# Feed-forward stage of a streaming encoder step: paced weight sums, operands of the first down steps on other bytes, sample columns stored apart, sums moved to POOL

## The chip, the cores and the metric

The kernel runs on one core of one Trainium2 chip. The metric is the device time of one execution in microseconds. Before the change the median of three runs is 1256.84 us (1256.39 to 1259.03). The engines are PE (TensorE, matrix products), DVE (VectorE), ACT (ScalarE), POOL (GpSimd) and SP (SyncE, which here issues the DMA transfers). Each engine works through its own instructions in order; they wait for one another by semaphores.

## The reference, cut to what matters

One layer of a hybrid encoder is computed for 1024 prompt frames and 8 × 16 sample frames: windowed attention and a state-space branch, an output projection, and then a feed-forward block with a short convolution. Only this last block is touched by the change:

```python
def conv_ffn(x, prev, w_up, conv_w, conv_b, w_down):
    up = x @ w_up                                        # 1152 rows, 1024 -> 2 * 2816
    up_p = jnp.concatenate([prev.astype(up.dtype), up], axis=1)
    c = sum(up_p[:, j:j + L] * conv_w[j] for j in range(CONV_W)) + conv_b
    gate, val = jnp.split(c, 2, axis=-1)
    return (jax.nn.silu(gate) * val) @ w_down, up_p[:, -(CONV_W - 1):]

x = x + f                                                # then the final rmsnorm
```

All tensors are float32. The last two rows before the convolution are an output too (conv_prompt, conv_sample).

## The kernel before

**Precision and products.** Every float32 operand is split into a high part (ACT: a copy to fp32r) and a low part (DVE: source minus high part); a product is three matmuls, high × high, high × low and low × high (`mm3`, lines 61 to 63). Every DVE tensor_tensor goes through the helper `tt`, so all of them stand at line 86 and are told apart by their tiles. Both matrix products of the block use a Strassen-like scheme: seven products of blocks in place of eight, with sums and differences of operands formed beforehand.

**Up stage.** The loop at line 1451 runs over 22 pairs j. A pair is 128 gate columns and 128 value columns. `load_up` brings its weights in (tiles `ur`, three buffers, 512 KB each). `prep(n)` makes operand n = 7j + i: POOL forms the sums of weights (`S`, and in place in `ur`, line 1253), ACT and DVE split them into `op` (lines 1297 and 1298). It runs seven operands, one pair, ahead of the products. `product(n, g)` does 12 matmuls for each of two groups of token tiles (g = 0: 320 columns, g = 1: 256) into PSUM tiles `pu{j}{g}{bank}`. `collect` moves the results to the row buffer `ext`, by ACT copies (line 1357) or DVE adds. `up_pair_end(j - 1)` does the convolution (`up_conv`: ACT line 1387, DVE lines 1388 and 1389), the SiLU (line 1394) and the product of gate and value, and stores the finished rows g to DRAM (`g_d`, line 1398): 1024 prompt columns and 144 columns of the samples (8 × (16 + 2)).

**Weight sums.** The down stage needs four sums of blocks of w_down. They are formed during the up stage, in 22 chunks: `wd_load(i)` loads four blocks of 256 columns into the one buffer `ws` (two DMAs, line 1414), `wd_sums(i)` does four DVE subtractions in place and stores the chunk to `t_d` (line 1424). In the loop the sums of chunk j - 1 are written at i == 0 and the load of chunk j at i == 3. Because `ws` has one buffer, a load has to wait until the store before it has landed.

**Down stage.** After the up stage its pools are closed, and new ones take the same bytes: `gr0` and `dwA` on the left, where the up weights (`upW`), the operands `op` with i < 3 (`opL`) and the split activations of group 0 (`hA`) lay, in this order, and `gr` and `dw` on the right. Seven passes of 11 steps follow (B11, T1, T2, B22, T3, B21, T4). A step loads a block of weights (`w_op`, tiles `wd`, five buffers), splits it (`wh`, `wl`), splits a tile of g (`gh`, `gl`), and does 12 matmuls for four tiles of prompt rows (`dna`, `dnb`). The first pass (line 1601) also takes the sample columns: four weight blocks a step, and 12 more matmuls for the 128 sample rows (`dns`). Two loads a step bring the sample columns of g (`gs`, line 1497). The pass for T1 needs `SU[k]`, the sum of two g tiles: `sum_one`, on DVE. `conv_out` transposes the convolution's last rows on PE (`cvo`, line 1549) and writes them out. `half_one` and `half_two` do the final normalization of a tile; for the samples they are written in pass T2 at step 3, and `final_g` (`fgb`) is loaded in T1 at step 9.

**What sets the order.** The program is written in one order, and a planner with a cost model then puts each engine's instructions into the order in which it expects them to be ready; the written order is the priority among ready ones. `with tc.issue_after(x):` adds an edge: the instructions of the block that run on the engine of x are queued behind x. It adds no semaphore. A tile of a pool can be written when all accesses of the tile that had its bytes are done.

Of the kernel before, what the change touches and what calls it, by code (L numbers as in the profile page):

```python
# [18 lines left out]
P = 128  # L19
# [26 lines left out]
def emit(ctx, tc, x_prompt, x_sample, cache_k, cache_v, state_ssm_re, state_ssm_im, state_conv,  # L46
# [1221 lines left out]
    RAW, OPS = {}, {}  # L1268

    def load_up(j):  # L1270

        if j < NF:
            for i in range(2):
                raw = upW.tile([P, 2, 4, P], F32, name=f"ur{j}{i}", tag="ur", bufs=3)
                c = i * DF + j * P
                nc.sync.dma_start(raw, w_up[0, :, c:c + P].rearrange("(h k p) n -> p h k n", p=P, h=2))
                RAW[j, i] = raw
# [6 lines left out]
    def prep(n):  # L1284
# [13 lines left out]
        tt(op[:, 1], src, f(op[:, 0]), OP.subtract)  # L1298
# [68 lines left out]
    g_d = dram.tile([NF, P, GLEN], F32, name="g_d")  # L1367
# [23 lines left out]
    def up_pair_end(j):  # L1391
# [6 lines left out]
        nc.sync.dma_start(g_d[j], g)  # L1398
# [52 lines left out]
    for j in range(1, NF):  # L1451
        load_up(j + 1)
        up_begin(j)
        for i in range(7):
# [7 lines left out]
            if i == 0:  # L1462
                wd_sums(j - 1)
            if i == 3:
                wd_load(j)
# [20 lines left out]
    def load_g(h, q, k):  # L1486

        if k < NK:
            pl = gr0 if h == q == 0 and k < 4 else gr
# [40 lines left out]

    load_g(0, 0, 0)
    load_g(0, 0, 1)
    load_gs(0)
    load_g(0, 0, 2)
    load_g(0, 0, 3)
    load_gs(1)
    for k in range(NK):
        SU[k] = None
# [59 lines left out]


    smb = {}  # L1600
    for k in range(NK):
        w = {}
        for blk in ("B11", "B12", "B21", "B22"):
            w[blk] = w_op(blk, k)
            if blk == "B11":
                g = g_op(GA[0, 0, k])
                pairs("a", k, g, w[blk], True)
                if k == 0:
                    smb = {e: pdn.tile([P, 512], F32, name=f"dns{e}", tag=f"b{2 + e}") for e in range(2)}
                sm = []  # L1610
                for q in range(2):
                    v = GS[q, k].rearrange("p (b s) -> p b s", s=NS + 2)[:, :, 2:]
                    hi, lo = (dwA.tile([P, P], F32R, name=f"s{x}{q}{k}", tag=f"s{x}{q}", bufs=2) for x in "hl")
                    hv, lv = (z.rearrange("p (b s) -> p b s", s=NS) for z in (hi, lo))
                    act(hv, v, AF.Copy)
                    tt(lv, v, f(hv), OP.subtract)
                    sm.append((hi, lo))
# [135 lines left out]
```

## Time and profile before

| | |
|---|---|
| median of 3 runs | 1256.84 us |
| profiled execution, its own time | 1257.5 us |
| its span in the profile | 1255.7 us |
| mean granted clock of TensorE | 0.974 |
| busy PE / DVE / ACT / POOL | 93% / 75% / 52% / 18% |
| up stage, pairs 2 to 20, in the span | 504.6 to 957.6 us |
| last matmul of the up stage ends | 986.35 us |
| last matmul of the down stage ends | 1242.3 us |

A row of a timeline holds the start in us, the duration in us, engine, line, operation, tiles (out<-in), shapes, how many were merged, and in brackets the idle time of the engine before it with what ended it. In a row of a chain the start is followed by the duration and what worked. A row of a table by windows holds the window and its length, then the busy time (and number of instructions) of PE, PEld (weight loads into PE), DVE, ACT and POOL, the granted clock of TensorE, the busy share of the DMA engines and GB/s. A row of a group holds line, engine, operation, tiles, shapes, count, then busy us, mean ns of one, and the idle time just before them with its causes. DMA issues stand at SPq. PE's rows overlap a little, since matmuls are pipelined; the distance between starts is the true pace. The span counts from the first instruction, and the execution's own time is a little longer.

### The profile page before, as it was taken

How to read it: one execution, taken by the hardware profiler on the slowest of the kernel's cores; microseconds unless marked ns; L12 is line 12 of the kernel's file. 1: busy time of each engine (PE TensorE's matmuls, PEld its weight loads, DVE VectorE, ACT ScalarE, POOL GpSimd, SP SyncE). 2: the span in 40 equal slices, each digit the busy share in tenths (PEclk: the TensorE clock that was granted, in tenths of full speed). 3: DMA queues.
4: the chain of work that ended last, by engine and by line, in shares of the span. 5: the costliest groups of instructions: out<-in, count | busy, mean ns of one | idle time of the engine just before them, and what ended most of it. 6: DMA issues, size and time to landing. Idle time of an engine off the chain costs nothing.

```text
span 1255.7 us, 20729 instructions
## 1 busy us (share of the span) xinstructions
PE 1172.0 (93%) x7396; PEld 1031.3 (82%) x7396; DVE 945.7 (75%) x2159; ACT 653.2 (52%) x1414; POOL 228.3 (18%) x276
## 2 busy tenths in 40 slices
PE   8999999999979878998899889999999899999995
PEld 6777776777878678998899889999999777888884
DVE  6898778888258888777787787776767669977666
ACT  7346557653467675443444344545454455546553
POOL 0000000000000114333443345553634000000000
PEclk9999999999999888999999999999999899999998
DMA  7523247638622433354534452212222499943333
GB/s 249 106 99 106 96 110 221 202 129 239 202 72 99 154 101 102 121 172 147 161 121 161 140 162 73 87 63 81 70 73 70 154 312 327 332 135 94 100 92 134
DMA packets 163945, 177.90 MB, mean 142 GB/s; under 512 B 30554, under 2 KB 121314, under 8 KB 163810
## 3 DMA queue, kind: packets, MB, share of 16 engines
q1 hardware_dynamic: 163842, 176.58, 44.7%
q8 instruction: 58, 0.95, 0.3%
q14 instruction: 45, 0.37, 0.1%
HBM read 124.36 MB, written 53.23 MB: 141 GB/s over the span
## 4 chain that ended last, share of the span: by engine, by line
PE 53%; DVE 19%; DMA 15%; issue 5%; ACT 5%; SPq 3%; POOL 1%; DVEq 0%; ACTq 0%; POOLq 0%
DMA ws<-in_w_down_dram 5%; DMA t_d<-ws 5%; PE dna L62 3%; PE dna L63 3%; PE dna L61 3%; PE dnb L63 2%; DVE op L86 2%; PE dnb L61 2%; PE dnb L62 2%; PE po L61 2%; PE po L62 2%; PE po L63 2%; DVE ws L86 2%; DVE cg L1389 1%; DMA wd<-in_w_down_dram 1%
## 5 line engine op out<-in xcount | busy, mean ns | idle before, releaser
L86 DVE TENSOR_TENSOR op<-ur,op 128x512 fp32r<-128x512 f32 x132 | 114.8, 871 | 61.1 <-ACT op L1297 59.7
L1297 ACT ACTIVATE op<-ur 128x512 fp32r<-128x512 f32 x132 | 81.9, 632 | 112.7 <-POOL ur L1253 74.7
L86 DVE TENSOR_TENSOR ws<-ws 128x256 f32<-128x256 f32 x88 | 40.6, 461 | 62.5 <-DMA ws<-in_w_down_dram 61.7
L1253 POOL TENSOR_TENSOR S<-ur 128x512 f32<-128x512 f32 x22 | 41.0, 1862 | 237.8 <-DMA ur<-in_w_up_dram 237.1
L1513 ACT ACTIVATE wh<-wd 128x512 fp32r<-128x512 f32 x110 | 68.9, 630 | 27.1 <-PE dnb L63 7.7
L86 DVE TENSOR_TENSOR wl<-wd,wh 128x512 fp32r<-128x512 f32 x110 | 74.6, 685 | 7.8 <-ACT wh L1513 7.6
L62 PE MATMUL dna<-wl,gh 128*128 128x512 f32 x176 | 70.0, 401 | 0.7 <-DVE wl L86 0.7
L61 PE MATMUL dna<-wh,gh 128*128 128x512 f32 x176 | 64.0, 398 | 2.1 <-ACT wh L1513 2.0
L1385 POOL COPY cvt<-ext 128x2 f32<-128x2 f32 x44 | 25.9, 588 | 197.0 <-DVE ext L86 197.0
L1387 ACT ACTIVATE cg<-ext,cw 128x1168 f32<-128x1168 f32 x22 | 30.0, 1364 | 55.8 <-DVE ext L86 55.8
L63 PE MATMUL dna<-wh,gl 128*128 128x512 f32 x176 | 55.8, 399 | 0.0
L62 PE MATMUL dnb<-wl,gh 128*128 128x512 f32 x132 | 50.5, 390 | 1.3 <-DVE wl L86 1.3
L86 DVE TENSOR_TENSOR gl<-gr,gh 128x512 fp32r<-128x512 f32 x44 | 30.3, 690 | 27.9 <-PE dna L63 10.9
L1513 ACT ACTIVATE gh<-gr 128x512 fp32r<-128x512 f32 x44 | 27.6, 630 | 44.2 <-PE dna L62 31.2
L61 PE MATMUL dnb<-wh,gh 128*128 128x512 f32 x132 | 50.3, 391 | 0.1
L1389 DVE SCALAR_TENSOR_TENSOR cg<-ext,cw,cg 128x1168 f32<-128x1168 f32 x22 | 44.8, 2034 | 0.0
L1386 POOL COPY cvt<-ext 128x16 f32<-128x16 f32 x44 | 35.1, 797 | 47.3 <-ACT ext L1357 47.3
L62 PEld LDWEIGHTS dna<-wl,gh 128*128 128x128 f32 x176 | 34.1, 194 | 8.7 <-DVE wl L86 1.4
L61 PEld LDWEIGHTS dna<-wh,gh 128*128 128x128 f32 x176 | 33.3, 191 | 9.7 <-ACT wh L1513 2.9
L63 PEld LDWEIGHTS dna<-wh,gl 128*128 128x128 f32 x176 | 34.2, 194 | 7.3
L1513 ACT ACTIVATE gh<-su 128x512 fp32r<-128x512 f32 x33 | 20.9, 633 | 36.2 <-PE dna L62 16.4
L1253 POOL TENSOR_TENSOR ur<-S,ur 128x512 f32<-128x512 f32 x22 | 33.5, 1524 | 31.9 <-DVE op L86 30.5
(1276 smaller groups left out, 4358.7 us busy)
## 6 DMA issues: line engine op xcount, KB each, us to landing
ur<-in_w_up_dram SPq DMA_DIRECT2D x44, 512.0 KB, 4.7
wd<-in_w_down_dram SPq DMA_DIRECT2D x66, 256.0 KB, 3.9
g_d<-g SPq DMA_DIRECT2D x22, 584.0 KB, 2.9
ws<-in_w_down_dram SPq DMA_DIRECT2D x44, 256.0 KB, 3.5
t_d<-ws SPq DMA_DIRECT2D x22, 512.0 KB, 3.3
gr<-g_d SPq DMA_DIRECT2D x44, 256.0 KB, 4.9
wd<-t_d SPq DMA_DIRECT2D x44, 256.0 KB, 3.4
wa<-a_d SPq DMA_DIRECT2D x9, 512.0 KB, 3.8
```

Of the source, the lines that this page charges most:

```text
L61: mm(out, lh, rh, start=first, stop=False, skip_group_check=True)
L62: mm(out, lh, rl, start=False, stop=False, skip_group_check=True)
L63: return mm(out, ll, rh, start=False, stop=last, skip_group_check=True)
L86: V_.tensor_tensor(o, a, b, op=op)
L1253: nc.gpsimd.tensor_tensor(o, a, b, op=op)
L1297: act(op[:, 0], src, AF.Copy)
L1385: nc.gpsimd.tensor_copy(cvt[:, 0:2, ft], ext[:, SEQ:SEQ + 2])
L1386: nc.gpsimd.tensor_copy(cvt[:, 2:, ft].rearrange("p (b j) -> p b j", j=2), es[:, :, NS:])
L1387: act(o, ext[:, 2:], AF.Identity, bias=cw[:, 3, ft:ft + 1], scale=cw[:, 2, ft:ft + 1])
L1389: stt(o, ext[:, 0:GLEN], cw[:, 0, ft:ft + 1], o, op0=OP.mult, op1=OP.add)
L1513: act(hi, src, AF.Copy)
```

## The change

Five things are done.

1. In the loop over pairs, `wd_sums(j - 1)` stands at i == 1 and is tied behind the low part (DVE) of the operand seven products ahead; `wd_load(j)` stands at i == 4 and is tied behind the last load of up weights of pair j + 1 (SP).
2. `gr0` holds three tiles instead of four, and the first two steps of the B11 pass allocate their tiles first, so that they lie on the bytes of `upW` and `opL`. The prompt's products of steps 0 and 1 are written before any sample product; step 1 then does the sample products of steps 0 and 1. The transposes of `conv_out` move from step 2 to step 4, tied behind the step's last prompt matmul.
3. The 144 sample columns go to a DRAM tensor of their own (`gs_d`), by a second store a pair, and come back in four loads of three steps each in place of 22.
4. `sum_one` runs on POOL. The first three sums are written at steps 8 to 10 of the first pass.
5. The samples' normalization moves from T2 to T3, the load of `final_g` from T1 to T2.

```diff
 def load_up(j):
-                nc.sync.dma_start(raw, w_up[0, :, c:c + P].rearrange(...))
+                UR[j] = nc.sync.dma_start(raw, w_up[0, :, c:c + P].rearrange(...))
 def prep(n):
-        tt(op[:, 1], src, f(op[:, 0]), OP.subtract)
+        LOW[n] = V_.tensor_tensor(op[:, 1], src, f(op[:, 0]), op=OP.subtract)
...
-    g_d = dram.tile([NF, P, GLEN], F32, name="g_d")
+    g_d = dram.tile([NF, P, SEQ], F32, name="g_d")
+    gs_d = dram.tile([P, NF, GLEN - SEQ], F32, name="gs_d")
 def up_pair_end(j):
-        nc.sync.dma_start(g_d[j], g)
+        nc.sync.dma_start(g_d[j], g[:, 0:SEQ])
+        nc.sync.dma_start(gs_d[:, j], g[:, SEQ:])
 for j in range(1, NF): for i in range(7):
-            if i == 0:
-                wd_sums(j - 1)
-            if i == 3:
-                wd_load(j)
+            if i == 1:
+                with tc.issue_after(LOW[min(n + 7, 7 * NF - 1)].ins):
+                    wd_sums(j - 1)
+            if i == 4:
+                with tc.issue_after(UR[min(j + 1, NF - 1)].ins):
+                    wd_load(j)
 def load_g(h, q, k):
-            pl = gr0 if h == q == 0 and k < 4 else gr
+            pl = gr0 if h == q == 0 and k < 3 else gr
 def load_gs(k):
-        if k < NK:
+        if k < NK and k % 3 == 0:
+            n = min(3, NK - k)
+            t = dwA.tile([P, 2, 3, GLEN - SEQ], F32, name=f"gs{k}", tag="gs", bufs=2)
+            nc.sync.dma_start(t[:, :, 0:n], gs_d.rearrange("p (q k) c -> p q k c", q=2)[:, :, k:k + n])
             for q in range(2):
-                GS[q, k] = dwA.tile([P, GLEN - SEQ], F32, name=f"gs{q}_{k}", tag=f"gs{q}", bufs=3)
-                nc.sync.dma_start(GS[q, k], g_d[q * NK + k, :, SEQ:])
+                for i in range(n):
+                    GS[q, k + i] = t[:, q, i]
...
-    load_g(0, 0, 0)
-    load_g(0, 0, 1)
-    load_gs(0)
-    load_g(0, 0, 2)
-    load_g(0, 0, 3)
-    load_gs(1)
+    for k in range(3):
+        load_g(0, 0, k)
+    def sum_one(k):
+        if k < NK:
+            SU[k] = gr.tile([P, 512], F32, name=f"su{k}", tag=f"su{k}")
+            nc.gpsimd.tensor_tensor(SU[k], GA[1, 0, k], GA[1, 1, k], op=OP.add)
+    def p1_pairs(k):
+        w11[k] = w_op("B11", k)
+        g = g_op(GA[0, 0, k])
+        for p in range(NP2):
+            c = slice(p * P, (p + 1) * P)
+            last = mm3(bank("a", p, k == 0), g[0][:, c], g[1][:, c], *w11[k], k == 0, k == NK - 1)
+        return last
+    def p1_sample(k):
...
+        for blk in ("B11", "B12", "B21", "B22"):
+            w = w11[k] if blk == "B11" else w_op(blk, k)
...
     for k in range(NK):
...
+        last = p1_pairs(k)
+        if k == 1:
+            load_gs(0)
+            load_g(0, 0, 3)
+            for i in range(2):
+                p1_sample(i)
+        elif k:
+            p1_sample(k)
+        if k:
+            with tc.issue_after(WD[0].ins):
+                load_g(0, 0, k + 3)
+                load_gs(k + 2)
+                if k >= 5:
+                    load_g(1, 0, k - 5)
+                    load_g(1, 1, k - 5)
+                if k == 4:
+                    load_x(NPT)
+        if k == 4:
+            with tc.issue_after(last.ins):
+                conv_out()
+        if k >= 8:
+            sum_one(k - 8)
...
-    for k in range(3):
-        sum_one(k)
 pass T1:
-            if k == 9:
-                nc.sync.dma_start(fgb, bcast_row(final_g, DM))
 pass T2:
+            if k == 9:
+                nc.sync.dma_start(fgb, bcast_row(final_g, DM))
-        if k == 3:
-            half_one(NPT, LO)
-            half_two((NPT,), LO, HI)
 pass T3:
+        if k == 3:
+            half_one(NPT, LO)
+            half_two((NPT,), LO, HI)
```

More of the change, by code (lines that the diff above doesn't have):

```diff
@@ L1267, in emit @@
     upW = h2s.enter_context(pool("upW"))
-    RAW, OPS = {}, {}
+    RAW, OPS, UR, LOW = {}, {}, {}, {}
     def load_up(j):
@@ L1275, in load_up @@
                 c = i * DF + j * P
-                nc.sync.dma_start(raw, w_up[0, :, c:c + P].rearrange("(h k p) n -> p h k n", p=P, h=2))
+                UR[j] = nc.sync.dma_start(raw, w_up[0, :, c:c + P].rearrange("(h k p) n -> p h k n", p=P, h=2))
                 RAW[j, i] = raw
@@ L1529, in g_op @@
         return operand(src, "g", CG, 2, spare)
-    load_g(0, 0, 0)
-    load_g(0, 0, 1)
-    load_gs(0)
-    load_g(0, 0, 2)
-    load_g(0, 0, 3)
-    load_gs(1)
-    for k in range(NK):
-        SU[k] = None
+    for k in range(3):
+        load_g(0, 0, k)
     def conv_out():
@@ L1597, in pairs @@
             mm3(bank(x, p, opens and k == 0), g[0][:, c], g[1][:, c], *w, opens and k == 0, k == NK - 1)
-    smb = {}
-    for k in range(NK):
[L1602 to L1617, printed above, removed]
-            q, e = int(blk[1]) - 1, int(blk[2]) - 1
-            mm3(smb[e], *sm[q], *w[blk], k == 0 and q == 0, k == NK - 1 and q == 1)
-        with tc.issue_after(WD[0].ins):
-            load_g(0, 0, k + 4)
-            load_gs(k + 2)
-            if k >= 5:
-                load_g(1, 0, k - 5)
-                load_g(1, 1, k - 5)
-            if k == 4:
-                load_x(NPT)
-        if k == 2:
-            conv_out()
@@ new lines, in sum_one @@
+    def sum_one(k):
+        if k < NK:
+            SU[k] = gr.tile([P, 512], F32, name=f"su{k}", tag=f"su{k}")
+            nc.gpsimd.tensor_tensor(SU[k], GA[1, 0, k], GA[1, 1, k], op=OP.add)
+    smb, w11 = {}, {}
+    def p1_pairs(k):
[6 more added lines that the diff above has]
+    def p1_sample(k):
+        sm = []
+        for q in range(2):
+            v = GS[q, k].rearrange("p (b s) -> p b s", s=NS + 2)[:, :, 2:]
+            hi, lo = (dwA.tile([P, P], F32R, name=f"s{x}{q}{k}", tag=f"s{x}{q}", bufs=2) for x in "hl")
+            hv, lv = (z.rearrange("p (b s) -> p b s", s=NS) for z in (hi, lo))
+            act(hv, v, AF.Copy)
+            tt(lv, v, f(hv), OP.subtract)
+            sm.append((hi, lo))
+        if k == 0:
+            for e in range(2):
+                smb[e] = pdn.tile([P, 512], F32, name=f"dns{e}", tag=f"b{2 + e}")
+        for blk in ("B11", "B12", "B21", "B22"):
+            w = w11[k] if blk == "B11" else w_op(blk, k)
+            q, e = int(blk[1]) - 1, int(blk[2]) - 1
+            mm3(smb[e], *sm[q], *w, k == 0 and q == 0, k == NK - 1 and q == 1)
@@ L1632, in emit @@
         tt(o, o, smb[e], OP.add)
-    def sum_one(k):
-        if k < NK:
-            SU[k] = gr.tile([P, 512], F32, name=f"su{k}", tag=f"su{k}")
-            tt(SU[k], GA[1, 0, k], GA[1, 1, k], OP.add)
-    for k in range(3):
-        sum_one(k)
     for k in range(NK):
```

## The prediction

> **What bounds the kernel now.** I read the page first, its span and the busy time of each engine.
>
> ```profile
> span 1255.7 us, 20729 instructions
> PE 1172.0 (93%) x7396; PEld 1031.3 (82%) x7396; DVE 945.7 (75%) x2159; ACT 653.2 (52%) x1414; POOL 228.3 (18%) x276
> ```
>
> TensorE is the bound of the whole, so time can only come out of stretches where it stands still or is clocked down. Next I looked at when each feed-forward pair begins its first product on PE (timeline of PE, three moments), for the pace of a pair.
>
> ```profile
> 504.62 0.31 PE L61 MATMUL pu20a<-hh,op 128*128 128x320 f32 x1
> ...
> 757.39 0.31 PE L61 MATMUL pu120a<-hh,op 128*128 128x320 f32 x1
> ...
> 957.58 0.31 PE L61 MATMUL pu210a<-hh,op 128*128 128x320 f32 x1
> ```
>
> Pairs 2 to 11 take (757.39 − 504.62) / 10 = 25.28 us each; pairs 12 to 20, with the same matmuls, (957.58 − 757.39) / 9 = 22.24 us. Ten pairs lose 3.04 us each, 30.4 us in all. The windows of the two stretches, the groups of DVE in each (first one row of pairs 2 to 11, then one of pairs 13 to 20) and a piece of the chain of waits say why.
>
> ```profile
> 504.62:757.39 252.77, 229.54 (x1683) 225.07 (x1681) 190.23 (x288) 104.38 (x217) 99.83 (x121) 0.99 0.47 147
> 780.04:957.58 177.54, 177.54 (x1346) 177.54 (x1345) 126.22 (x170) 88.72 (x176) 87.87 (x96) 1.00 0.22 72
> ...
> L86 DVE TENSOR_TENSOR ws<-ws 128x256 f32<-128x256 f32 x78 | 35.3, 453 | 60.9 <-DMA ws<-in_w_down_dram 60.2
> ...
> L86 DVE TENSOR_TENSOR op<-ur,op 128x512 fp32r<-128x512 f32 x48 | 43.5, 907 | 49.9 <-ACT op L1297 48.8
> ...
> 663.95 3.40 DMA ws<-in_w_down_dram
> ...
> 668.81 3.59 DMA t_d<-ws
> ...
> 673.00 3.12 DMA ws<-in_w_down_dram
> ...
> 546.54 0.39 PE L61 MATMUL pu31a<-hh,op 128*128 128x256 f32 x1 [1.15 <-ACT ext L1357]
> ```
>
> The weight sums run as a ring through one buffer: load 3.4 us, four sums, store 3.6 us, next load. About two chunks go through a pair (78 sums in ten pairs), and VectorE, which works in order, stands still for 60.2 us until their loads land. ScalarE then finds its inputs late, its copy out of PSUM is late, and PE waits for that copy, as in the last row. Without chunks (pairs 13 to 20) PE is busy for the whole window at a granted clock of 1.00.
>
> The third place is the step from the up stage to the down stage: rows of PE's timeline around 986 and 1025, then the last matmul, two rows of the chain ten steps apart, and the windows.
>
> ```profile
> 986.07 0.28 PE L63 MATMUL pu211c<-hh,op 128*128 128x256 f32 x1
> 987.58 0.47 PE L1549 MATMUL cvo<-ident,cvt 128*88 128x128 f32 x2 [1.23 <-POOL cvt L1385]
> ...
> 990.22 0.47 PE L1549 MATMUL cvo<-ident,cvt 128*128 128x128 f32 x1 [1.62 <-DVE cvr L1551]
> 990.35 2.05 PE L61 MATMUL dna<-wh,gh 128*128 128x512 f32 x4
> ...
> 999.17 0.40 PE L63 MATMUL dns<-wh,sl 128*128 128x512 f32 x1
> ...
> 1025.24 1.20 PE L61 MATMUL dna<-wh,gh 128*128 128x512 f32 x4 [2.02 <-ACT wh L1513]
> ...
> 1241.87 0.40 PE L63 MATMUL dna<-wh,gl 128*128 128x512 f32 x1
> ...
> 1184.01 0.91 PE dnb L63 x4
> ...
> 1211.21 0.91 PE dnb L63 x4
> ...
> 990.00:1015.00 25.00, 24.07 (x89) 18.68 (x90) 20.07 (x37) 12.82 (x26) 0.00 (x0) 0.82 0.71 234
> 1015.00:1040.00 25.00, 22.98 (x95) 18.50 (x94) 16.96 (x33) 13.50 (x28) 0.00 (x0) 0.93 0.94 303
> 1040.00:1065.00 25.00, 23.57 (x103) 18.89 (x102) 22.57 (x39) 13.65 (x26) 0.00 (x0) 1.00 0.97 328
> 1065.00:1090.00 25.00, 24.68 (x108) 19.95 (x108) 25.00 (x51) 13.03 (x23) 0.00 (x0) 1.00 0.92 324
> ...
> L1549 PE MATMUL cvo<-ident,cvt 128*128 128x128 f32 (+2 forms) x7 | 1.9, 322 | 3.1 <-DVE cvr L1551 1.8 <-POOL cvt L1385 1.2
> ```
>
> A step of twelve matmuls takes (1211.21 − 1184.01) / 10 = 2.72 us, 0.227 us a matmul. The down stage has 7 × 11 steps and 11 more for the sample columns: 88 × 2.72 = 239.4 us. With 1.9 us for the transposes of the convolution output it would end 241.3 us after the last up matmul at 986.35, at 1227.6; it ends at 1242.3. So 14.7 us are lost, and nearly all of it before 1090. From 986.35 to the row after 999.17 (999.40), 13.05 us pass for 19 matmuls (4.3 us) and four transposes (1.1 us): 7.6 us lost to gaps and to half speed (four matmuls in 2.05 us, granted clock 0.82 in that window). Around 1025 it is 2.2 us of gap and eight matmuls 0.2 us too slow each: 3.8 us. The remaining 3.3 us lie mostly at the start of T1, near 1061 to 1070.
>
> **The change part by part.**
>
> Paced sums: the four subtractions of a chunk are tied behind the low part of the operand seven products ahead, their load behind the last up-weight load of its pair, so one chunk goes through each of 22 pairs. The load gets nearly a whole pair; it needs 3.4 us, so the 60 us of VectorE's waits should go. The sums themselves (4 × 0.453 = 1.8 us) now also lie in pairs 12 to 21. There VectorE idles 49.9 us in eight pairs for ACT's operands alone, 6.2 us a pair: the cover. If that cover were gone, a pair would lose up to 1.8 us. The pace that is left is that of pairs 12 to 20, if nothing else stalls: gain 30.4 us at most. I take off 0.1 us for each of some 20 pairs, 2 us: **28.5 us**. Bounds: 30.4, and 0 if each chunk costs PE as much as now (30.4 us over 78 / 4 chunks is 1.6 us a chunk). I choose near the upper end because the row of VectorE puts its waits on the loads and not on the sums. The last chunk's sums and 1 MB of traffic fall into the end of pair 21, where DMA has room.
>
> On SP each t_d store waits for the sums and the next load for the store's landing, and the up-weight loads and g stores queue behind them.
>
> ```profile
> 831.33 3.33 SPq L1276 DMA_DIRECT2D ur<-in_w_up_dram  x2
> 846.11 0.34 SPq L1398 DMA_DIRECT2D g_d<-g  x1
> ...
> 837.27 1.39 DVE L86 TENSOR_TENSOR op<-ur,op 128x512 fp32r<-128x512 f32 x1
> ...
> 840.97 0.69 DVE L86 TENSOR_TENSOR op<-ur,op 128x512 fp32r<-128x512 f32 x1
> ```
>
> These rows (SP, then VectorE's splits of the first two operands of pair 16) lie in pair 15, a pair without chunks; it begins near 757.39 + 3 × 22.24 = 824.1. The up weights go out 7 us into the pair, the sums would follow the second split, 17.5 us into it, and SP would then stand blocked for some 4 us of store, past which only the g store has to go. I cost it at nothing. If an up load were caught, it would come some 4 us late; the first operand is ready at 838.7, 7.7 us before pair 16 begins near 846.4.
>
> Sample columns apart: one more store a pair, 0.34 us of SP, hidden as SP idles there. In the first pass of the down stage four loads replace 22, 18 issues less, each of about the same 0.34 us of SP. The bytes are the same, so DMA gets nothing from it. Cost zero; gain between 0 and 1.
>
> First two steps early: operands for steps 0 and 1 lie where the up weights and left operands were, free long before the last product. Today the second down-weight load waits for that last product and ACT reaches the down weights only behind the convolution of pair 21:
>
> ```profile
> 977.93 8.30 SPq L1525 DMA_DIRECT2D wd<-in_w_down_dram  x4
> ...
> 986.17 1.36 ACT L1387 ACTIVATE g<-ext,cw 128x1168 f32<-128x1168 f32 x1
> ...
> 989.47 2.18 ACT L1513 ACTIVATE wh<-wd 128x512 fp32r<-128x512 f32 x4
> ...
> L86 DVE TENSOR_TENSOR wl<-wd,wh 128x512 fp32r<-128x512 f32 x58 | 39.1, 685 | 6.7 <-ACT wh L1513 6.6
> ...
> L1388 DVE SCALAR_TENSOR_TENSOR cg<-ext,cw,cg 128x1168 f32<-128x1168 f32 x1 | 1.4, 1424 | 0.0
> ```
>
> 24 matmuls (5.4 us) can then follow pair 21 directly, while the rest loads (some 4 us from 985) and is split. Five VectorE operations of pair 21's convolution, 5 × 1.42 = 7.1 us, still compete with the splits of the first sample steps (three weights, 3 × 0.685 = 2.1 us, each), so I leave 2.5 us of the 7.6 standing: **gain 5**, bounds 0 and 7.6. Moving the transposes to step 4 takes their 3.1 us of waiting out of the bare transition; their own time stays.
>
> Does the slow clock go? After waits of 1.2 and 1.6 us the matmuls ran at half speed for 9 us. The Trainium skill (TensorE: Matmul & The Clock Gate, Part 1, What's actually happening) has the clock drop only after an idle window of about 3.4 us. By that rule gaps as short as these would not be what slows PE, closing them would win 4 us less, and the sum would come to 1226; the rows of 1.23 and 1.62 us of waiting followed by four matmuls in 2.05 us speak against it.
>
> The DMA of the first pass is the limit to this: shares of 0.94 and 0.97 while PE runs near its pace. The wait at 1025 comes from a down-weight load that took twice its usual time behind a 512 KB x load.
>
> ```profile
> 1007.22 4.03 DMA wd<-in_w_down_dram
> ...
> 1016.75 7.71 DMA wd<-in_w_down_dram
> ```
>
> The change keeps the x load at step 4 and puts a triple sample load (442 KB) beside it. I expect this stall to stay: gain **0**, between −3.8 (it doubles) and +3.8.
>
> Gated sums on POOL: eleven sums leave VectorE, which is full (25.00 of 25) in T1 and waits for late gr loads in order. POOL's time for this shape is bounded by its own rows:
>
> ```profile
> 835.62 2.49 POOL L1253 TENSOR_TENSOR S<-ur 128x512 f32<-128x512 f32 x1
> ...
> L1253 POOL TENSOR_TENSOR ur<-ur 128x512 f32<-128x512 f32 x22 | 29.2, 1329 | 2.3 <-DVE op L86 1.4
> ```
>
> POOL takes 1.3 to 2.5 us, under the 2.72 us of a step; a VectorE split of the same shape beside it took 1.39 us instead of 0.69 (rows at 837.27 and 840.97). So each sum moved saves 0.69 us and costs about 0.7. That is no gain of work, only of waiting: the sums' late loads no longer block VectorE. With the sample's norm taken out of T1 and T2 (hidden in T3, whose PE has no gaps), I take **1.5 us** of the 3.3, bounds −9 (eleven sums of which each delays VectorE by 0.8 us net) and 3.3. The Trainium skill (SBUF — State Buffer, Who interferes with whom) says that VectorE with two SBUF inputs and a reading GpSimd lock each other out. The 1.39 us agree; by it alone this part would gain nothing, and the sum would be 1223.5.
>
> Sum: 28.5 + 5 + 0 + 1.5 = 35. Span 1255.7 − 35 = 1220.7; the profiled execution took 1257.5, 1.8 us around its span, so 1222.5. It lies 0.7 above the median of 1256.84, so **1222 us**; its own range is 1214 to 1231.
>
> **The rivals.**
>
> 1. The transition gives nothing: the splits of steps 0 and 1 are queued on ACT and VectorE behind pair 21's convolution as now, and DMA keeps the pass at its pace (or the gaps close and the slow clock stays, 1226). For: ACT's rows at 986 to 991, DMA share 0.97. Against: VectorE and ACT have room before 986. Time: 1222 + 6.5 = 1228.5.
> 2. The pacing does only half: chunks in every pair leave one PSUM copy late per pair. For: PE waits after ACT's ext copies twice a pair now, 1.15 us and more each time, with two chunks. Against: the loads are early. At 1.3 us in 20 pairs: 1222 + 26 = 1248; at half of it 1235.
> 3. T1 becomes VectorE's: POOL's sums slow it, +9 us: 1222 + 1.5 + 9 = 1232.
> 4. Slower than before: SP, blocked by a store that waits for the sums and a load that waits for the store, lets the up weights go late, and all of pairs 2 to 21 run as pairs 2 to 11 do today. Then pairs 12 to 21 lose 3.04 us each where they lost nothing: 1256.8 + 30.4 − 6.5 = 1281. It decides from (30.4 + 6.5) / 20 = 1.85 us lost a pair. For: SP works in order, and in pairs with chunks the first operand is later. Against: the row at 831.33, 7 us into its pair, far from the sums.
>
> **How the numbers follow.** Main case 0.60, first rival 0.17, second 0.11, third 0.06, fourth 0.06. From 1212 to 1240 lie the main case, the first and third and about half of the second: some 0.87, less a little for a gain beyond the upper bounds. Same means within 0.2%, 2.5 us, what a measurement here can tell. Faster 0.92 (all but the fourth and a tail of the second), same 0.02, slower 0.06.
>
> **What would show it.** Right: pairs 2 to 20 begin 22.2 to 22.5 us apart; VectorE's wait for ws near zero; the first dna matmuls directly behind pu211c, the first window of the down stage at a clock above 0.95; a gap near step 5 with a wd load over 6 us. Wrong: pairs above 23.5 us; ws still waited for; PE idle over 1 us before the first dna; VectorE operations of 1.4 us through T1 with PE waiting on wl or gl.

## The result and the profile after

The changed kernel takes **1226.21 us** (median of 4 runs, 1225.34 to 1227.28), the kernel before 1256.62 us on the same chip: a ratio of 0.9765 (95% interval 0.9731 to 0.98). The profiled execution took 1226.02 us, its span is 1223.9. Its span and busy times, from the page:

```profile
span 1223.9 us, 20731 instructions
PE 1161.8 (95%) x7396; PEld 1024.3 (84%) x7396; DVE 953.9 (78%) x2148; ACT 657.3 (54%) x1414; POOL 253.2 (21%) x287
```

PE's timeline gives the moments that were read before: the starts of pairs 2, 12 and 21, the last matmul of the up stage and the first of the down stage, two waits in the first pass (B11), the first of T1 and a wait behind it, the first of T2, and the last matmul of all.

```profile
503.14 0.31 PE L61 MATMUL pu20a<-hh,op 128*128 128x320 f32 x1
...
725.07 0.31 PE L61 MATMUL pu120a<-hh,op 128*128 128x320 f32 x1
...
924.81 0.31 PE L61 MATMUL pu210a<-hh,op 128*128 128x320 f32 x1
...
953.30 0.28 PE L63 MATMUL pu211c<-hh,op 128*128 128x256 f32 x1
955.43 1.20 PE L61 MATMUL dna<-wh,gh 128*128 128x512 f32 x4 [1.85 <-ACT wh L1521]
956.88 0.80 PE L62 MATMUL dna<-wl,gh 128*128 128x512 f32 x1 [0.25 <-DVE wl L86]
957.48 0.63 PE L63 MATMUL dna<-wh,gl 128*128 128x512 f32 x1
957.90 0.63 PE L62 MATMUL dna<-wl,gh 128*128 128x512 f32 x1
...
968.34 0.96 PE L61 MATMUL dna<-wh,gh 128*128 128x512 f32 x3 [0.82 <-ACT wh L1521]
...
978.30 0.50 PE L61 MATMUL dns<-wh,sh 128*128 128x512 f32 x1 [1.44 <-ACT wh L1521]
...
1024.62 0.73 PE L61 MATMUL dnb<-wh,gh 128*128 128x512 f32 x2 [0.72 <-ACT wh L1521]
1027.64 0.50 PE L62 MATMUL dnb<-wl,gh 128*128 128x512 f32 x1 [2.29 <-DVE wl L86]
...
1060.17 0.39 PE L61 MATMUL dna<-wh,gh 128*128 128x512 f32 x1
...
1209.73 0.39 PE L63 MATMUL dna<-wh,gl 128*128 128x512 f32 x1
```

All pairs now begin 22.19 us apart, (725.07 − 503.14) / 10 and (924.81 − 725.07) / 9, where the first ten took 25.28. From pair 2 to the last up matmul it is 450.2 us instead of 481.5: **31.3 us gained**. The group of the weight sums on VectorE and the table by windows of the ten pairs show the cause: the wait for ws, 60.2 us before, is 0.2 us for all 22 chunks (88 sums), and PE is busy throughout the ten pairs. A window's row begins with its limits and length; the numbers behind POOL's are the granted clock, the DMA share and GB/s. The last three rows are the start of the down stage, 25 us more of its first pass, and pass T1.

```profile
L86 DVE TENSOR_TENSOR ws<-ws 128x256 f32<-128x256 f32 x88 | 54.0, 613 | 0.8 <-DVE ext L86 0.4 <-DMA ws<-in_w_down_dram 0.2
...
503.14:725.04 221.90, 221.90 (x1682) 221.90 (x1681) 179.67 (x250) 110.63 (x220) 109.94 (x120) 1.00 0.38 120
953.58:978.58 25.00, 20.64 (x80) 15.77 (x81) 20.52 (x36) 15.98 (x31) 0.86 (x2) 0.93 0.80 256
978.58:1003.58 25.00, 24.09 (x108) 18.98 (x108) 18.80 (x40) 14.53 (x30) 3.01 (x2) 1.00 0.98 340
...
1024.62:1060.17 35.55, 32.73 (x132) 25.30 (x133) 34.98 (x62) 15.73 (x28) 7.78 (x5) 0.95 0.85 301
```

The down stage won nothing. The two rows below are the first of T1 and the first of T2 in the kernel before.

```profile
1059.63 0.39 PE L61 MATMUL dnb<-wh,gh 128*128 128x512 f32 x1
...
1091.37 0.39 PE L61 MATMUL dna<-wh,gh 128*128 128x512 f32 x1
```

Counted from the start of the last up matmul to the end of the span it takes 1223.85 − 953.30 = 270.6 us, before 1255.72 − 986.07 = 269.7. Pass T1 (1024.62 to 1060.17) takes 35.56 us instead of 32.65 us. (There T2's first eight matmuls run ahead of T1's last four, so 0.91 us for these four are added to the 31.74 us between the two rows.) In the window above VectorE is busy for 34.98 of 35.55 us. The five later passes last 29.9 us each in both kernels. The difference of the two spans is then complete: 1.5 us from an earlier start of pair 2 (503.14 for 504.62, which no edit explains), 31.3 from the pairs, 2.2 up to T1's start, −2.9 in T1 and −0.2 behind it, 31.9 in all. (Each is read from one profile of each kernel.)

### The profile page after: what moved, and what is told of

The parts are those of the page before. It is cut to its first block, busy times and chain, and to the rows that moved or that the text cites. A ratio compares the mean times of both kernels' runs of the same rounds, so it can differ in the third digit from the quotient of the medians.

```text
span 1223.9 us, 20731 instructions
## 1 busy us (share of the span) xinstructions
PE 1161.8 (95%) x7396; PEld 1024.3 (84%) x7396; DVE 953.9 (78%) x2148; ACT 657.3 (54%) x1414; POOL 253.2 (21%) x287
## 5 line engine op out<-in xcount | busy, mean ns | idle before, releaser
L1298 DVE TENSOR_TENSOR op<-ur,op 128x512 fp32r<-128x512 f32 x132 | 121.6, 924 | 83.6 <-ACT op L1297 83.4
L1386 POOL COPY cvt<-ext 128x2 f32<-128x2 f32 x44 | 30.3, 688 | 158.4 <-DVE ext L86 158.4
L86 DVE TENSOR_TENSOR ws<-ws 128x256 f32<-128x256 f32 x88 | 54.0, 613 | 0.8 <-DVE ext L86 0.4
L1253 POOL TENSOR_TENSOR ur<-S,ur 128x512 f32<-128x512 f32 x22 | 36.5, 1658 | 18.7 <-DVE op L1298 18.7
L1253 POOL TENSOR_TENSOR ur<-ur,ur 128x512 f32<-128x512 f32 x22 | 37.9, 1721 | 1.7
```

The costliest lines, as they stand in the source:

```text
L86: V_.tensor_tensor(o, a, b, op=op)
L1253: nc.gpsimd.tensor_tensor(o, a, b, op=op)
L1298: LOW[n] = V_.tensor_tensor(op[:, 1], src, f(op[:, 0]), op=OP.subtract)
L1386: nc.gpsimd.tensor_copy(cvt[:, 0:2, ft], ext[:, SEQ:SEQ + 2])
```

## The experiments

The start of pair 2 lies between 499.4 and 505.5 us in all profiles here, whatever was edited, so medians of two of these kernels that are less than some 3 us apart say little. Therefore each run is read also from the last up matmul onward. The ratio is that of the mean times, to the kernel before on the same chip, whose medians beside the runs were 1256.6 (after), 1254.7 (e1 to e4), 1252.8 (e5 to e8), 1252.9 (e9 to e11) and 1252.4 us (e12). The other columns are read off PE's timeline, in us; first dna, T1 and end of span count from the start of the last up matmul. Where T2 begins ahead of T1's last four matmuls (before, e2, e5), these are added to T1.

| run | median us | ratio to before (95%) | pairs 2 to 11 | first dna | T1 begins | T1 takes | end of span |
|---|---|---|---|---|---|---|---|
| before | 1256.62 | | 25.28 | 4.28 | 73.56 | 32.65 | 269.65 |
| after | 1226.21 | 0.9765 (0.9731 to 0.98) | 22.19 | 2.13 | 71.31 | 35.56 | 270.55 |
| e1 no pacing | 1259.52 | 1.0039 (1.0022 to 1.0056) | 25.35 | 2.03 | 70.02 | 36.28 | 269.98 |
| e2 pacing only | 1221.72 | 0.9733 (0.9714 to 0.9751) | 22.19 | 4.28 | 70.18 | 32.95 | 266.58 |
| e3 chunk early | 1227.66 | 0.9776 (0.9758 to 0.9793) | 22.19 | 2.02 | 71.94 | 35.31 | 270.94 |
| e4 sums on DVE | 1223.08 | 0.9737 (0.9717 to 0.9758) | 22.19 | 2.02 | 72.10 | 33.97 | 269.76 |
| e5 first pass only | 1223.92 | 0.9765 (0.975 to 0.9781) | 22.19 | 2.19 | 70.08 | 32.32 | 267.18 |
| e6 late differences | 1222.14 | 0.9752 (0.9726 to 0.9778) | 22.19 | 2.03 | 70.96 | 32.22 | 266.87 |
| e7 one block | 1218.57 | 0.9743 (0.9706 to 0.978) | 22.19 | 2.29 | 70.19 | 31.40 | 266.19 |
| e8 one block, pacing | 1221.44 | 0.9744 (0.9723 to 0.9765) | 22.19 | 4.27 | 69.15 | 31.56 | 264.21 |
| e9 splits first | 1225.18 | 0.9779 (0.9761 to 0.9797) | 22.19 | 0.12 | 71.62 | 34.35 | 269.66 |
| e10 pacing, late | 1221.36 | 0.9749 (0.9731 to 0.9767) | 22.19 | 4.27 | 70.45 | 31.83 | 265.74 |
| e11 combined | 1217.85 | 0.9725 (0.9699 to 0.9751) | 22.19 | 0.12 | 68.08 | 31.89 | 263.66 |
| e12 x later | 1220.83 | 0.9747 (0.9729 to 0.9765) | 22.19 | 0.12 | 68.20 | 31.84 | 263.71 |

Most intervals of the paced kernels overlap: e5's ratio, for example, is the changed kernel's. Where these kernels are compared below, the stretches are of one profile each, and differences of some tenths of a microsecond between them carry no weight.

### Which part did it: e1 and e2

e1 is the changed kernel with the old places of the sums, e2 the kernel before with the paced sums alone:

```diff
 e1:
-            if i == 1:
-                with tc.issue_after(LOW[min(n + 7, 7 * NF - 1)].ins):
-                    wd_sums(j - 1)
-            if i == 4:
-                with tc.issue_after(UR[min(j + 1, NF - 1)].ins):
-                    wd_load(j)
+            if i == 0:
+                wd_sums(j - 1)
+            if i == 3:
+                wd_load(j)
 e2: the same lines the other way round, in the kernel before
```

> The change without its pacing: sums at i == 0 and loads at i == 3 again, every other part kept. Theory A (SP's queue: in the changed kernel the first down-weight load stands behind the ring of the last chunk) expects pairs 2 to 11 at 25.3 us again, but no chunk at the end, so that the first down-weight load goes out some 8 us before the last up matmul, PE goes on without a gap, and the stretch from the last up matmul to the span's end falls from 270.3 us to about 265: 1251 us. Theory B (the step is held by ACT, VectorE and DMA, whatever SP's order) expects the first dna matmul 1.5 us or more behind the last up matmul and that stretch at 270: 1257 us.

> The kernel before with the paced sums alone. The up stage should run at 22.2 us a pair, 31 us faster. If the other four parts are worth nothing beside the pacing, as the profile after suggests, this takes 1226 us too, within 1.5. If they hide a gain or a loss in the down stage (the stretch behind the last up matmul was 269.3 us before and 270.3 after), it differs by that: with theory A the ring of the last chunk stands in front of the down stage's first loads here too, and the stretch is 270 to 273 us, 1226 to 1229.

Without the pacing the other four parts make the kernel slower, by 0.39% (0.22 to 0.56), near 5 us; its profile does not show where, since its span (1255.9 us) is the one of the profile before (1255.7). Its first dna comes 2.03 us behind the last up matmul and its last stretch takes 269.98 us, as theory B expected. The pacing alone gives 33 us (1254.7 us was the kernel before beside it), and the end of its down stage comes 4 us earlier than in the full change, although its first dna matmul comes 2.1 us later: the other four parts hide a loss. Three rows of its PE timeline, the second at step 5, then a window of the kernel before behind its wait at step 5 (1025.24):

```profile
953.09 0.28 PE L63 MATMUL pu211c<-hh,op 128*128 128x256 f32 x1
...
990.48 0.73 PE L61 MATMUL dna<-wh,gh 128*128 128x512 f32 x2 [0.46 <-ACT wh L1515]
...
1023.27 0.61 PE L61 MATMUL dnb<-wh,gh 128*128 128x512 f32 x2
...
1026.42:1029.83 3.41, 3.41 (x10) 2.62 (x9) 2.58 (x6) 0.79 (x3) 0.00 (x0) 0.50 0.92 277
```

Its T1 begins 70.18 us behind the last up matmul, with the old step between the stages, while before the change it was 73.56. The 3.4 us lie at step 5. PE waits 0.46 us there instead of 2.02, and the stretch at a granted clock of 0.50 (half clock) that follows this wait in the kernel before, 3.41 us long, does not come; it costs up to half its length, 1.7 us, and 1.6 + 1.7 = 3.3. The transition itself is the same in both (4.28 us). Why the wait is shorter is not shown: with one profile of each kernel it can be the pacing or the scatter of the loads. Scatter is likely a part of it, since the two profiles' spans are 36.0 us apart and the medians 33.0.

### The step between the stages: e3 and e9

In the changed kernel SP issues the first wd load only behind the store of the last chunk, which waits for the sums:

```profile
950.52 0.56 SPq L1426 DMA_DIRECT2D t_d<-ws  x1
951.13 1.62 SPq L1533 DMA_DIRECT2D wd<-in_w_down_dram  x2
```

One theory was that this queue holds the first step back, the other that ACT's order does. e3 moves every chunk one pair forward, so that nothing of the ring is left behind the loop:

```diff
+    wd_load(0)                       # ahead of pair 0's second group; its sums and load 1 at i == 5
 for j in range(1, NF): ...
-                    wd_sums(j - 1)
+                    wd_sums(j)
-                    wd_load(j)
+                    wd_load(j + 1)   # if there is one
-    wd_sums(NF - 1)
```

> The change with every chunk one pair earlier: the first is loaded before pair 0's second half and summed in it, the last is summed in pair 21 at i == 1, and nothing of the ring is left behind the loop. Theory A expects the first down-weight load right behind the g stores of pair 20, some 8 us before the last up matmul, the first dna within 0.5 us of it, and 4 to 6 us less: 1221 us. Theory B expects 1226 within 1.

Its rows (SP, PE, then ACT):

```profile
943.78 1.28 SPq L1534 DMA_DIRECT2D wd<-in_w_down_dram  x2
...
952.48 0.28 PE L63 MATMUL pu211c<-hh,op 128*128 128x256 f32 x1
954.50 1.19 PE L61 MATMUL dna<-wh,gh 128*128 128x512 f32 x4 [1.75 <-ACT wh L1522]
...
951.54 1.15 ACT L1522 ACTIVATE gh<-gr 128x512 fp32r<-128x512 f32 x2
952.58 1.36 ACT L1388 ACTIVATE g<-ext,cw 128x1168 f32<-128x1168 f32 x1
953.83 0.62 ACT L1522 ACTIVATE wh<-wd 128x512 fp32r<-128x512 f32 x1
```

The loads go out 8.7 us before the last up matmul, and the first dna waits as long as it did. The SP theory falls. What stands in front of wh is the convolution of pair 21, because ACT's order was fixed with it there. e9 adds to e3 the other order: the high parts of step 0 stand ahead of pair 21's last copies, those of step 1 ahead of its convolutions (edges of issue order only).

```diff
+        if k == 1:
+            queue_behind(HI_["g", 1], HI_["w", 0])
+        if k < 2:
+            for x in "wg":
+                for i in range(2):
+                    queue_behind(CONV[NF - 1, i], HI_[x, k])   # ACT's part of up_conv(21, i)
+                if k == 0:
+                    for e in EVIC[7 * NF - 2, 1]:              # the last copies ext<-pu211a
+                        queue_behind(e, HI_[x, 0])
```

> The changed kernel with each chunk of weight sums a pair earlier, and with ACT's order changed by hand at the end of the up stage: the high parts gh and wh of step 0 stand ahead of pair 21's last copy out of PSUM, those of step 1 ahead of its two convolutions. With the early chunks alone the first dna matmul still came 2.02 us behind the last up matmul, on a wh that stood behind the convolution. If ACT's order is what is left of the transition's wait, the first dna comes within 0.6 us, without the half-speed matmuls behind it (some 2 to 3 us), and the stretch from the last up matmul to the end falls from 270.9 to 266.5 to 269; the median is 1222 to 1225. If first dna comes early but T1 begins as late as before (71 to 72 us behind the last up matmul), the first pass takes the gain back, and the time stays within 1.5 us of 1227.7. If first dna stays at 2 us, ACT's order is not the cause.

```profile
954.00 0.28 PE L63 MATMUL pu211c<-hh,op 128*128 128x256 f32 x1
954.11 1.31 PE L61 MATMUL dna<-wh,gh 128*128 128x512 f32 x4
...
990.00 1.19 PE L61 MATMUL dna<-wh,gh 128*128 128x512 f32 x4 [2.82 <-ACT wh L1522]
...
1025.61 0.73 PE L61 MATMUL dnb<-wh,gh 128*128 128x512 f32 x2 [0.25 <-ACT wh L1522]
```

The first dna follows the last up matmul directly and the wait is gone: ACT's order was its cause. But T1 begins 71.62 us behind it, where it was 71.94 in e3 and 71.31 in the changed kernel. PE stands 2.82 us at step 5, for a wh whose load was issued behind the x load. The gain at the start of the pass was lost inside it: two stretches of 3.41 us at half clock lie in this pass too, the second behind this wait.

### What holds the first pass: e5, e7, e8, e12

e5 keeps parts 1 to 3 only; parts 4 and 5 are undone.

```diff
-            nc.gpsimd.tensor_tensor(SU[k], GA[1, 0, k], GA[1, 1, k], op=OP.add)
+            tt(SU[k], GA[1, 0, k], GA[1, 1, k], OP.add)
-        if k >= 8: sum_one(k - 8)           # first pass
+    for k in range(3): sum_one(k)          # behind it
 half_one, half_two of the samples: T3 -> T2; load of final_g: T2 -> T1
```

> The changed kernel with its parts 4 and 5 undone: the eleven sums go back to VectorE and behind the first pass, the samples' normalization back to T2, the load of final_g back to T1. What is left are the paced sums, the early bytes and the separate sample columns. Pass T1 took 32.65 us before, 35.56 us after the change, 33.97 us with the sums on VectorE alone. If parts 4 and 5 are what lengthened T1, T1 takes 32.5 to 33.2 us here, and the median is 1222 to 1223.5, level with the pacing alone (1221.7): the early bytes and the separate columns are then worth nothing together. If T1's loss comes out of the reordered first pass, T1 stays at 34 us or more and the time at 1223 to 1225.

T1 is back at 32.32 us, so parts 4 and 5 had lengthened it. T1 begins at 70.08 us, the pacing alone has 70.18: the early bytes and the separate columns together show no gain there (0.1 us). (T2 took 31.01 us in e5 and 30.81 in e7, 29.9 in all others; that was not followed up.)

e7 and e8 leave out three of four weight loads of the first pass, e7 in the changed kernel and e8 in the pacing alone. Three of the four sample products of a step then use the wrong weights, so the sample rows of these two kernels are not the reference's:

```diff
 def w_op(blk, k, spare=False): ...
+        if k in ONE and blk != "B11":       # first pass
+            return operand(RB[k], "w", CW, 4, spare)   # RB[k]: the raw block B11 of this step
...
```

> The changed kernel with less traffic in the first pass: of the four down-weight blocks a step only the first is loaded, and it is split four times in place of the other three. The sample rows of the result thereby come from the wrong weights; the work of ACT, VectorE and PE is the same, 8.4 MB of loads are left out. The first pass takes 69.18 us in the changed kernel, its matmuls alone 60. If the pass is bound by its loads, and that is where the two us gained at its start were lost again, it takes 61 to 64 us and the median falls to 1218 to 1221. If it is bound by the order of the splits on ACT and VectorE, it stays at 68 us or more and the time within 1.5 us of 1226.

> The pacing alone (the old first pass) with the same loads left out. Its first pass takes 65.90 us with all loads and begins 4.28 us behind the last matmul of the up stage, instead of 2.13. If the early bytes win their two us and the loads then take them back, T1 begins here 2 to 4 us later, counted from the last up matmul, than in the changed kernel with the same loads left out. If the early bytes win nothing in any case, T1 begins within 1 us of it.

Both expectations of a pass bound by its loads missed. With 8.4 MB less the passes end only 1.1 us (71.31 to 70.19) and 1.0 us (70.18 to 69.15) earlier. (e7's median, 1218.57 us, lies in the range named for a pass bound by loads, but through an early pair 2, at 499.36, and a short T1.) The waits change their owner. Late in e7's pass the longest two are no longer for wd but for VectorE's wl, and VectorE is nearly full; first two rows of its PE timeline, then a window of the first pass:

```profile
989.28 0.50 PE L62 MATMUL dns<-wl,sh 128*128 128x512 f32 x1 [0.85 <-DVE wl L86]
...
992.17 0.50 PE L62 MATMUL dna<-wl,gh 128*128 128x512 f32 x1 [0.91 <-DVE wl L86]
...
974.80:999.80 25.00, 22.96 (x102) 17.75 (x101) 23.46 (x40) 13.03 (x28) 11.01 (x6) 1.00 0.72 251
```

The g tiles land sooner there, POOL makes six of the sums in this window (11.01 us busy), and VectorE works beside it for 23.46 of 25 us. Nor do the early bytes show a gain of their own with the loads gone: e7's T1 begins 1.04 us later than e8's.

e12 is e11 (below) with the x load of 512 KB at step 8 instead of step 4, to see whether this load is the stall that was found at step 5.

```diff
-                if k == 4:
+                if k == 8:
                     load_x(NPT)
```

> The run of the combined edits (early chunks, ACT's order by hand, late differences, four tiles in gr0), with the 512 KB load of the samples' residual rows (x) written at step 8 of the first pass instead of step 4. There the loads behind it landed 6 to 7 us after their issue, and PE stood 1.49 us for a wh of step 5, 2.82 us in the run with ACT's order alone. If this load beside the triple sample load is what holds the first pass, the wait at step 5 falls below 0.5 us, T1 begins at 64.5 to 67 us behind the last up matmul instead of 68.08, and the median is 1214 to 1217. If the loads as a whole are too much for these steps, a wait of 1 us or more stands at step 5 or one step later, and the time stays within 1 us of 1217.85.

```profile
955.65 0.28 PE L63 MATMUL pu211c<-hh,op 128*128 128x256 f32 x1
...
1006.36 0.50 PE L61 MATMUL dna<-wh,gh 128*128 128x512 f32 x1 [0.86 <-ACT wh L1522]
...
1023.85 0.50 PE L61 MATMUL dnb<-wh,gh 128*128 128x512 f32 x1 [0.43 <-ACT wh L1522]
```

The wait at step 5 is gone, another of 0.86 us stands at step 8, and T1 begins at 68.20 us where it was 68.08. The weights of that second wait were issued ahead of the x load, which SP issues only at 1005.59. So the x load carried the wait at step 5, but it is not what holds the pass. (The profiles' spans differ by 2.4 us, of which 2.3 lie ahead of pair 2, in work that the two have in common.)

The 264 matmuls of the first pass need 264 × 0.227 = 59.9 us at full pace, in all kernels. What is on top, from the last up matmul to T1, are gaps and late steps, which are distances between matmul starts of over 0.05 us more than 0.227, idle time taken off: 5.79 us of gaps and 33 late steps before (6.4 us), 6.31 and 29 (4.3 us) after, 4.19 and 23 (4.7 us) in e2, 5.05 and 28 (4.4 us) in e7, 3.42 and 25 (3.9 us) in e11; the rest, 0.8 to 1.5 us, was not split further. Half clock is only a part of the late steps: it lasts 13.65 us before, 10.24 in e2 and 3.41 us in each of the other three, where it can cost 1.7 us. No single wait carries these sums. The runs suggest that several limits lie close together here (loads, VectorE, ACT's order); which of them is the nearest at each step stays open.

### T1: e4, e6 and e10

e4 is the changed kernel with the sums on VectorE (the first two lines of e5's diff).

> The change with the gated sums on VectorE again (at the changed places). If POOL and VectorE hold each other up (VectorE's operations of 1.75 us near 1026 to 1034 beside POOL's sums), the start of T1 loses 2 us less: 1224. If POOL takes the load off VectorE, as the prediction had it (1.5 us): 1227.5. Same if both cancel: 1226.

T1 takes 33.97 instead of 35.56 us. How POOL's sums cost VectorE time is seen in the changed kernel, at the start of T1 (POOL, then VectorE):

```profile
1023.31 1.28 POOL L1604 TENSOR_TENSOR su<-gr,gr 128x512 f32<-128x512 f32 x1 [5.92 <-DMA gr<-g_d]
...
1024.62 0.69 DVE L86 TENSOR_TENSOR gr<-gr,gr 128x512 f32<-128x512 f32 x1 [2.90 <-POOL su L1604]
1025.23 0.68 DVE L86 TENSOR_TENSOR gl<-su,gh 128x512 fp32r<-128x512 f32 x1
1025.84 1.75 DVE L86 TENSOR_TENSOR wl<-wd,wh 128x512 fp32r<-128x512 f32 x1
```

gr<-gr,gr is the difference that pass B22 needs, three passes later. It overwrites a tile that the sum reads, and the planner has put it into the first pass. VectorE stands 2.90 us for it until POOL's sum is done, which itself had waited for its load, and the wl of T1's first step is queued behind: PE's wait of 2.29 us at 1027.64. Beside POOL that wl then takes 1.75 us. Two causes, then: waiting in order, and slower operations. e6 removes the first and leaves the sums on POOL:

```diff
+        with tc.issue_after(LO_[0].ins):     # the latest low part, on VectorE
             tt(GA[1, 0, k], GA[0, 0, k], GA[1, 0, k], OP.subtract)
```

> The changed kernel, with the eleven subtractions that pass B22 writes (gr<-gr,gr, on VectorE) tied behind that pass's own operand splits; nothing else. In the changed kernel the planner places them from step 9 of the first pass on, and VectorE stands in front of them for 1.96, 1.19 and 2.90 us, the last time for a sum on POOL. If that waiting in order is how POOL's sums cost time, T1 takes about 33 us instead of 35.56 and the time is 1223 to 1224. If it is VectorE being slowed beside POOL (operations of 1.75 us in place of 0.69), T1 stays above 35 us and the time within 1 us of 1226.

```profile
1022.50 0.62 PE L61 MATMUL dnb<-wh,gh 128*128 128x512 f32 x2
...
1054.72 0.39 PE L61 MATMUL dna<-wh,gh 128*128 128x512 f32 x1
```

T1 takes 32.22 us, as fast as with parts 4 and 5 undone (e5, 32.32), and the end of the span comes 3.7 us earlier than in the changed kernel. The waiting in order was most of the cost; operations of 1.2 to 1.8 us still stand in VectorE's row there, and PE does not wait for them as long. Half clock made the wait dearer: T1 of the changed kernel has a mean clock of 0.95 over 35.55 us, which is one stretch of 3.41 us at 0.50 (from 1028.18), up to 1.7 of the 3.3 us; e6's T1 has 1.00. e10 puts the same tie on the pacing alone.

> The pacing alone, with the differences for pass B22 tied behind that pass's operand splits, as in the run of the late differences. There this tie shortened T1 from 35.56 to 32.22 us, where sums on POOL made VectorE wait in front of them. Here the sums are on VectorE and T1 takes 32.95 us. If the tie helps only against the wait for POOL, T1 stays within 0.7 us of 32.95 and the time at 1221 to 1222.5. If the differences also crowd VectorE's own work in T1, T1 falls to 30.5 to 32 us and the time to 1219 to 1221.

T1 falls from 32.95 to 31.83 us, so the differences seem to crowd VectorE also without POOL. The time, 1221.36 us, does not differ from e2's by more than the runs scatter.

### What adds up: e11

e9 and e6 together, and four tiles in gr0 again, so that the g tile of step 3 is loaded with the first three (in the changed kernel it went out behind fourteen weight loads):

```diff
-            pl = gr0 if h == q == 0 and k < 3 else gr
+            pl = gr0 if h == q == 0 and k < 4 else gr
-    for k in range(3):
+    for k in range(4):
         load_g(0, 0, k)
-            load_g(0, 0, 3)                  # at k == 1
```

> The changed kernel with the early chunks, ACT's order by hand and the late differences together, and with four tiles in gr0 as before the change, so that the g tile of step 3 is loaded with the first three and not behind the first fourteen weight blocks. If the losses found so far are separate, they add up: T1's pass 32.2 us, first dna within 0.6 us, the wait of 1.2 to 1.5 us at step 3 gone; from the last up matmul to the end 262 to 265.5 us instead of 270.55, and the median 1217 to 1221, below the pacing alone (1221.7). If the first pass is held by something else, T1 begins at 70 us or later and the median is 1221 to 1223.

```profile
953.32 0.28 PE L63 MATMUL pu211c<-hh,op 128*128 128x256 f32 x1
953.44 0.39 PE L61 MATMUL dna<-wh,gh 128*128 128x512 f32 x1
...
987.92 0.50 PE L61 MATMUL dna<-wh,gh 128*128 128x512 f32 x1 [1.49 <-ACT wh L1522]
...
1021.40 0.39 PE L61 MATMUL dnb<-wh,gh 128*128 128x512 f32 x1
```

The end comes 263.66 us behind the last up matmul, 6.9 us earlier than in the changed kernel, and 1217.85 us (1215.08 to 1223.01, 5 runs) is the best median among the kernels that leave no work out, with a ratio of 0.9725 (0.9699 to 0.9751). This does not set it apart from the pacing alone by time, since e2 has 0.9733 (0.9714 to 0.9751) and e12, with the x load alone moved, 0.9747. In the profiles e11 and e12 end 2.1 and 2.0 us earlier than e10, the pacing with the late differences (265.74). So the other parts may win something once the orders on ACT and VectorE are right and the g tile of step 3 is early; which edit carries how much was not separated.

## Why the prediction was right or wrong, point by point

**The time** was forecast as 1222 us (1212 to 1240) and is 1226.21. The sum was right in its large term and wrong in two small ones. That it came within 4.2 us is partly luck: the small terms, 6.5 us in the sum, came out as a loss of 0.9 (2.2 won up to T1, 3.1 lost from there on), the pairs gave 2.8 us more than priced, and 1.5 us came from an earlier start of pair 2 that no edit explains.

- **Paced sums, 28.5 us, bounds 0 to 30.4.** Right: 31.3 us in the pairs, and e2 has 33 us for this part alone. That is 0.9 us above the upper bound, which took the pace of pairs 12 to 20 as it was; they gained 0.05 us each as well. The 0.1 us a pair that was taken off for VectorE's crowding was not lost. The sums themselves became slower, 613 instead of 453 ns on average; 16 of the 88, which begin inside one of POOL's sums of up weights, took 1.5 us each, the others 0.41 to 0.43. That lay within VectorE's idle time, as the step had it. SP's blocking, priced at nothing, cost nothing: no up weights came so late that a pair slowed down (all stand 22.19 us apart), and the fourth rival (1281) is out.
- **Sample columns apart, 0.** Not measured by itself; with the early bytes it is 0.1 us in e5.
- **First two steps early, 5 us, bounds 0 to 7.6.** Wrong. The wait at the start shrank from 4.28 to 2.13 us, but against the pacing alone T1 begins 1.1 us later. The step failed at two points. It took for granted that the splits of steps 0 and 1 get ahead of pair 21's convolution once their bytes are free; ACT's order was planned with the convolution in front (e3, e9). And it counted a gain at the start of the pass as a gain at its end; e9 shows that with the whole wait gone T1 begins no earlier. The first reason of the first rival, splits queued behind the convolution as now, is what happened, and its 1228.5 is 2.3 us off on the other side. Its second, that DMA keeps the pass at its pace, is not borne out: without 8.4 MB of loads the pass ends 1.1 us earlier (e7). The last chunk's sums and its 1 MB, for which the prediction saw room in DMA, did hold back SP (first wd load 2.2 us ahead of the last up matmul, 8.7 in e3), but this decided nothing.
- **The stall near step 5, 0, bounds −3.8 to 3.8.** In the changed kernel there is no wait at step 5; waits of 0.7 to 1.4 us stand at 968, 978 and 984, all for weights issued ahead of the x load (979.97). In e9 and e11 step 5 waits 2.82 and 1.49 us for weights issued behind the x load, as the prediction read it before, and in e12 that wait goes with the load. But T1 begins no earlier in e12, and in e2 the wait is 0.46 us with the x load where it was. So no gain came, as forecast, but not because the stall stayed: it was replaced by others.
- **Sums on POOL and the sample norm later, 1.5 us, bounds −9 to 3.3.** Wrong in sign: T1 is 2.9 us longer and the tail 0.2. The sentence that failed is that the sums' late loads would no longer block VectorE. They did, through the differences for B22 that stand in its order and wait for the same sums (2.90 us in one row). The contention that the third rival priced was there (1.75 us in place of 0.69), but e6 shows that it was the smaller part: T1 is 3.3 us shorter with the sums still on POOL. The +9 us did not come. The rule of the Trainium skill that was weighed there (SBUF — State Buffer, Who interferes with whom: the two lock each other out) agrees with that row, and its result, no gain, was nearer than the forecast. The norm's move was not run by itself.
- **The slow clock.** The first window of the down stage has 0.93, where above 0.95 was forecast as a sign. The alternative that the Trainium skill gave (TensorE: Matmul & The Clock Gate, Part 1, What's actually happening: the clock drops only after some 3.4 us of idling) is not what the rows show: behind 1.85 us of waiting, matmuls start 0.42 us apart (957.48, 957.90), at a granted clock of 0.50.
- **Signs.** Pairs 22.19 us apart and no wait for ws were the marks of the main case and came. The gap near step 5 did not come. PE idle over 1 us before the first dna, and VectorE operations above 1.4 us with PE waiting on wl in T1, were named as marks of error; both came, and both belong to the terms that failed.

## What to carry to other kernels

A gain read from a wait at the head of a stage is a gain only if the stage behind it is not held by something else; compare the start of the stage after next, not the first matmul. A wait of PE can cost more than its length, when a stretch at half clock follows. Before work is moved to another engine, look which instructions on the old engine wait for its result in order, those that a planner has pulled forward for a much later pass included. A chain of load, sums and store through one buffer is cheap to pace and can cost 60 us of an engine's idling where it is not.

## What the runs showed of the hardware

- In these traces the clock follows PE's busy share, not single gaps. From 940 us to the last matmul, in all fourteen traces, the granted clock drops to 0.50 for 3.41 us or two or three times that, and the stretches of a trace lie on one grid of 3.41 us. Each drop follows a cell of that grid in which PE, by the profile's account, was busy for at most 52%; after every cell at full clock with 53% or more it stays at 1.00. So gaps of nearly one length have two outcomes. First two cells of the changed kernel, around its gap of 1.85 us (46%, then half clock), then one row and two cells of e1 (53%, then full clock):

```profile
953.09:956.50 3.41, 1.56 (x9) 0.96 (x7) 3.33 (x6) 3.41 (x4) 0.86 (x2) 1.00 0.99 277
956.50:959.91 3.41, 3.16 (x8) 2.45 (x8) 3.41 (x4) 2.60 (x8) 0.00 (x0) 0.50 0.92 338
...
987.98 1.19 PE L61 MATMUL dna<-wh,gh 128*128 128x512 f32 x4 [1.75 <-ACT wh L1519]
...
984.43:987.84 3.41, 1.81 (x15) 1.60 (x14) 2.58 (x6) 3.15 (x7) 1.08 (x3) 1.00 0.42 115
987.84:991.25 3.41, 2.90 (x11) 2.10 (x12) 3.41 (x4) 3.41 (x9) 0.00 (x0) 1.00 0.83 300
```

- Half clock can cost as much as the wait in front of it: at step 5 of the kernel before, a gap of 2.02 us is followed by 3.41 us at 0.50, up to 1.7 us more.
- A VectorE operation of two SBUF inputs on 128x512 took 0.67 to 0.69 us alone in the down stage of the changed kernel. Beside POOL's sums of the same shape it mattered which began first: seven that began just ahead of one took no longer, seven that began inside one took 0.78 to 1.78 us.
- Leaving out 8.4 MB of the first pass's loads lowered the DMA share in the window of e7 to 0.72, against 0.98 around the same place in the changed kernel, and moved T1's start by 1.1 us only.
